# A hybrid SSD and latent-attention decode step: the decay mask added ahead of a biased Exp, the norm weight moved into w_out, and the page table read whole in an earlier stage

## The chip, the cores and the metric

The kernel is one program on one core of a Trainium2 chip. A core has a matrix engine (TensorE, here PE, with its weight loads shown apart as PEld), three engines for the rest (VectorE or DVE, ScalarE or ACT, GpSimd or POOL), and SyncE (SP), which here issues most DMA transfers. Each engine works through its own instructions strictly in the order in which they stand, and waits on semaphores for the others. The metric is device time in microseconds (us) for one execution. Smaller is better. Before the change, the median of three timed runs was 2083.14 us (2076.83 to 2083.86).

## The reference, cut to what matters

Two layers run over a prompt of 1024 tokens and over 8 sequences of 8 new tokens each (64 tokens, the "sample"). Layer 0 is a Mamba-2 SSD mixer with 32 heads in 8 groups, layer 1 is multi-head latent attention (MLA) with a paged cache of 2048 past positions for each sequence. What the change touches of the SSD mixer:

```python
seg = a_cs[..., :, None] - a_cs[..., None, :]
decay = jnp.where(causal, jnp.exp(jnp.where(causal, seg, 0.0)), 0.0)
cb = jnp.einsum('bclgn,bcsgn->bgcls', cc, bc)
y_diag = jnp.einsum('bgrcls,bcsgrp->bclgrp', cb[:, :, None] * decay, xdt)   # xdt = x * dt
...
y = y.reshape(b, t, SSD_D_INNER) * jax.nn.silu(z.astype(F32))
yg = yg * lax.rsqrt(jnp.mean(yg * yg, axis=-1, keepdims=True) + NORM_EPS)
y = yg.reshape(b, t, SSD_D_INNER) * norm_w.astype(F32)
out = jnp.einsum('bte,ed->btd', y.astype(h.dtype), w_out)
```

So for each chunk of 128 tokens and each head, a 128x128 matrix of decays exp(a_cs[t] - a_cs[s]) is masked to s <= t, multiplied with the products of C and B, and multiplied into x * dt. Later the gated result is normalised by groups of 256, multiplied with `norm_w` for each of the 2048 columns, and projected by `w_out`. In layer 1 the sample's queries attend to pages that `page_table` (8 x 16 integers) names; the kernel fetches four pages of a sequence with one indirect transfer, for which each of the 128 partitions needs a row number: partition 32 j + r of item (b, q) needs page_table[b, 4 q + j] * 32 + r.

## The kernel before, in words

All products are made in a fast 32-bit format, with each operand split into a high part (a copy, on ACT) and a low part (the rest, a subtraction on DVE or POOL), and three products in place of one. The helper `split` (L129, L130) does that.

**Layer 0.** The eight SSD groups are handled one behind the other, as a pipeline of two: while `ssd_scan` goes over the nine token tiles of group g (eight of 128 prompt tokens, and the sample's 64), the generator `Group.steps` makes the projections of group g + 1. These are four convolution blocks of three pieces each (24 products into one of two PSUM buffers `pj`, evacuated by ACT at L452 to L455), convolved by DVE at L468, and a SiLU per pair of blocks at L429 (prompt, `acc`) and L430 (sample, `xs`), and then nine gate tiles `z` (L100). `layer_ssd` takes steps of the one as weights of the other allow, and within this a scheduler, which works from its own estimate of durations, lays out each engine's instructions. So the order on the engines isn't that of the code. Ahead of group 0, `ssd_dt` makes for each tile four columns per head in `k.tok`: 0 the cumulated decay exponent `acs`, 1 `dt`, 2 and 3 factors for the state and its output; it also writes `acs` transposed to DRAM as `acs_d`.

A tile of `ssd_scan` goes so. Transposes of x and B into `trp` (L537 to L540); ACT copies x to `xsT` (L542) and splits B; DVE makes `xdt` = x * dt (L555); POOL makes `xdd` = x times column 2 (L558), which is split with ACT's and POOL's help; POOL and ACT split the state S and C; POOL makes `xD` (L567). PE makes `pc` = B C (L569, PSUM tag `cb`, one buffer), and DVE multiplies it with the 0/1 mask into `cbm` (L571). A DMA broadcasts the tile's `acs` row of four heads to all partitions as `M` (L573, two buffers, 256 KB). DVE then does for each head `min(M - acs[s], 0)` (L575, four instructions of 128x128), ACT one Exp over all four heads (L577), DVE one product with `cbm` (L578). PE multiplies `M` with `xdt` into `py` (L582), makes the tile's state `st` (L586) and the part from the old state. DVE and POOL add up and gate `y` (L655 to L661), ACT sums its squares (L662), POOL multiplies it with the norm weight `nw` (L663), and SyncE writes it to `y_d`.

ACT keeps one table of functions at a time. Where Exp follows SiLU or the other way round, a table load stands ahead of it (ACT_TABLE_LOAD, under the line of the function that needs it).

The last group's scan has no projections beside it. Beside it runs `ssd_outproj` over the first eight of 16 row blocks of `w_out`, which `load_wout` loads, copies to `woh` on ACT (L703) and splits into `wol` on DVE and POOL in turn (L704). The second half of the blocks follows behind the scan. `rstd_of` scales with a power step on POOL (L204).

**Layer 1.** `mla_in` normalises the rows of the residual (`norm_steps`: transposes `xtp` with three PSUM buffers, then `hh` on ACT and `hl` on DVE, L235 and L236) and makes gates and latents; there `gather_kpe` fetches the page table as one number per partition (`kpidx`, L1353) and gathers key rows. Then `mla_q` makes the queries, with `Heads` already preparing the first heads, then `Sample.__init__` makes the row numbers: four transfers broadcast every fourth word of the page table to 32 partitions each (L1381), one loads r (`pslot`, L1383), and DVE converts, scales and converts back (L1385 to L1388). Then come the heads of the prompt, and the sample's attention, which uses the row numbers (`ptidx`) in 32 indirect transfers. In these last two stages PE and POOL keep the order of the code.

Of the kernel before, what the change touches and what calls it, by code (L numbers as in the profile page):

```python
# [18 lines left out]
NB = 8  # L19
# [18 lines left out]
SCALE = (NOPE + ROPE) ** -0.5  # L38
NEG = -1e30
GB = 4  # L40
NKT = 4
# [102 lines left out]
def ssd_tiles(k):  # L144
    cp, nc = k.cs, k.nc
    k.masku = cp.tile([128, 128], F32, name="masku")
    k.masks = cp.tile([64, 128], F32, name="masks")
    k.blkm = cp.tile([64, NB], F32, name="blkm")
    k.yssq = cp.tile([128, 9, G], F32, name="yssq")
# [13 lines left out]
def ssd_consts(k):  # L163
    nc, I = k.nc, k.I
    nc.sync.dma_start(k.masku, I["c_masku"])
    nc.sync.dma_start(k.masks, I["c_masks"])
    nc.sync.dma_start(k.blkm, I["c_blkm"])
    for j in range(3):
        nc.sync.dma_start(k.blk3[32 * j : 32 * j + 32], I["c_blkm"][:32, :4])
    nc.gpsimd.memset(k.yssq, 1.0)  # L170
    nc.sync.dma_start(k.dtb, I["ssd_dt_bias"][0].partition_broadcast(128))
    nc.sync.dma_start(k.dsk, I["ssd_d"][0].partition_broadcast(128))
# [162 lines left out]
def ssd_dt(k, pool, psum):  # L335
# [26 lines left out]
    def tokv(j):  # L362
        return k.tok[:, :, j]
# [3 lines left out]

    nc.gpsimd.tensor_copy(tokv(0), v(acs))
    nc.gpsimd.tensor_copy(tokv(1), v(dt))
    nc.vector.tensor_tensor(u, pt[:, :n], acs, op=ALU.subtract)  # L370
# [150 lines left out]
def ssd_scan(k, gr, pools):  # L521
# [4 lines left out]
    hs = slice(4 * g, 4 * g + 4)  # L526
    nw = sp.tile([128, 256], F32, tag="nw", name=f"nw{g}", bufs=1)
    nc.sync.dma_start(nw, I["ssd_norm_w"][0, 256 * g : 256 * g + 256].partition_broadcast(128))
    for i in ORDER[g]:
# [23 lines left out]

        xdt = sp.tile([128, 256], F32, tag="xdt", name="xdt" + tag, bufs=2)
        nc.vector.tensor_tensor(v3(xdt), v3(p[:, 0:256]), hb(1), op=ALU.mult)  # L555
        if not smp:
# [12 lines left out]
        nc.tensor.matmul(pc[:m, :m], B, C, start=True, stop=True)  # L569
        cbm = sp.tile([128, 128], F32, tag="cbm", name="cbm" + tag, bufs=1)  # L570
        nc.vector.tensor_tensor(cbm[:m, :m], pc[:m, :m], (k.masks if smp else k.masku)[:m, :m], op=ALU.mult)  # L571
        M = sp.tile([128, 4, 128], F32, tag="M", name="M" + tag, bufs=2)
        nc.sync.dma_start(M[:m, :, :m], (k.acss_d[hs] if smp else k.acs_d[i, hs]).partition_broadcast(m))  # L573
        for h in range(4):
            nc.vector.tensor_scalar(M[:m, h, :m], M[:m, h, :m], tk[:, 0, 4 * g + h : 4 * g + h + 1], 0.0,  # L575
                                    op0=ALU.subtract, op1=ALU.min)
        nc.scalar.activation(M[:m, :, :m], M[:m, :, :m], AF.Exp)  # L577
        nc.vector.tensor_tensor(M[:m, :, :m], M[:m, :, :m],  # L578
                                cbm[:m, :m].unsqueeze(1).to_broadcast([m, 4, m]), op=ALU.mult)
        py = psum.tile([128, 512], F32, tag="y", name="py" + tag, bufs=PB["y"])  # L580
        for h in range(4):
            nc.tensor.matmul(py[:m, h * 64 : h * 64 + 64], M[:m, h, :m], xdt[:m, h * 64 : h * 64 + 64],  # L582
                             start=True, stop=True)
# [78 lines left out]
        nc.scalar.activation(xD[:m], y[:m], AF.Square, accum_out=k.yssq[:m, i, g : g + 1])  # L662
        nc.gpsimd.tensor_tensor(y[:m], y[:m], nw[:m], op=ALU.mult)  # L663
        nc.sync.dma_start(k.y_d[sl, 256 * g : 256 * g + 256], y[:m])
# [30 lines left out]
def load_wout(k, pool, raws, kks, ws):  # L695
    nc = k.nc
    wo = k.I["ssd_w_out"][0]
    for kk in kks:
# [3 lines left out]
        nc.sync.dma_start(raw, wo[kk * 128 : kk * 128 + 128])  # L702
        nc.scalar.copy(hi, raw)  # L703
        (nc.vector if kk % 2 else nc.gpsimd).tensor_tensor(lo, raw, hi.bitcast(F32), op=ALU.subtract)  # L704
        ws.append((hi, lo))
# [161 lines left out]
def mla_in(k, right, mid):  # L867
    tc, nc, I = k.tc, k.nc, k.I
    k.g_d = k.dram.tile([8, 128, T], F32, name="g_d")
    with ExitStack() as st:  # L870
# [17 lines left out]
        with open_pool(tc, name="kg", bufs=1, side="right") as kg:  # L888
            gk = gather_kpe(k, kg)
            next(gk)  # L890
            for n in range(QG + 8):
                next(gates)
                if n >= QG:
                    next(gk)
# [477 lines left out]


class Sample:
    def __init__(self, k, pool):
        nc, I = k.nc, k.I
        self.k, self.sp = k, None
        pt = pool.tile([128, 32], mybir.dt.int32, name="ptab")
        for j in range(4):
            src = I["page_table"].rearrange("b (q j) -> j (b q)", j=4)[j : j + 1].to_broadcast([32, 32])  # L1380
            nc.sync.dma_start(pt[32 * j : 32 * j + 32], src)  # L1381
        ps = pool.tile([128, 1], F32, name="pslot")
        nc.sync.dma_start(ps, I["c_slot"])  # L1383
        pf = pool.tile([128, 32], F32, name="ptf")
        nc.vector.tensor_copy(pf, pt)  # L1385
# [409 lines left out]
def layer_mla(k):  # L1795
# [3 lines left out]
    with ExitStack() as st:  # L1799
# [27 lines left out]
        hd.open(heads, psum)  # L1827
        sm = Sample(k, qp)
        with tc.manual_schedule(engines={nc.tensor.engine, nc.gpsimd.engine}):
# [65 lines left out]
```

## Time and profile before

| | |
|---|---|
| timed runs | 2076.83, 2083.86, 2083.14 us, median 2083.14 |
| profiled execution | 2079.06 us, of which the span of the kernel's instructions is 2077.3 us |
| instructions on the chip | 33714 |
| PE busy | 1939.1 us, 93% of the span |
| DVE, ACT, POOL busy | 1325.8, 1043.0, 852.6 us |
| granted PE clock, mean | 0.977 of full speed |
| HBM traffic | 152.10 MB read, 53.28 MB written, 99 GB/s |

The profile is of one execution. Times in it count from the first instruction. A row of a group reads: line, engine, operation, output and inputs, shape, count, then busy time, mean duration in ns, and how long the engine stood idle ahead of it and what ended that. A row of the waits reads: engine and instruction, what it waited for, us in total, how often, longest. A row of the windows gives a stretch, with the busy time of PE, weight loads, DVE, ACT and POOL in it. Products on PE overlap, so their busy time is not PE at its peak.

The stages lie so: normalisation and the first group's projections up to 145 us, the scans of groups 0 to 6 up to about 840, the last scan with the first half of the output product up to about 1012, its second half up to about 1125, the input stage of layer 1 up to 1322, queries up to 1420, the prompt's heads up to about 1760, then the sample.

### The profile page before, as it was taken

What the parts mean: (1) busy time and instruction counts of PE and PEld (TensorE: products, weight loads), DVE (VectorE), ACT (ScalarE), POOL (GpSimd) and SP (SyncE); (2) the same over time, 40 slices, a digit from 0 to 9 for tenths busy, and PEclk for the clock granted to TensorE, in tenths of its full rate; (3) what the DMA queues carried; (4) which work ended last, traced back from release to release, by engine and by line L of the source; (5) the groups of instructions that cost most, each with busy time, mean ns of one, the idle gap of its engine ahead of it and who ended that gap; (6) DMA issues with size and microseconds to landing.
All of it is one profiled execution on the core that took longest, in us unless ns stands there. A gap on an engine that the chain in (4) does not pass through costs nothing.

```text
span 2077.3 us, 33714 instructions
## 1 busy us (share of the span) xinstructions
PE 1939.1 (93%) x12001; PEld 1750.3 (84%) x12001; DVE 1325.8 (64%) x2790; ACT 1043.0 (50%) x2288; POOL 852.6 (41%) x1059
## 2 busy tenths in 40 slices
PE   6999999999999999789998999799999999889998
PEld 5898989899999999677777998698888888778887
DVE  4558676767676768865434315366787868776665
ACT  5455555555565656522113314234676767755552
POOL 0337464646664646653000001102333434765541
PEclk9999999999999999889999999899999999999999
DMA  4222323232323241645544332132111212454451
GB/s 145 56 60 62 111 68 109 63 110 66 106 67 109 64 114 44 192 145 168 184 152 128 126 136 86 41 110 79 48 44 43 64 38 77 136 185 134 139 152 39
DMA packets 187631, 207.61 MB, mean 100 GB/s; under 512 B 23260, under 2 KB 153064, under 8 KB 187080
## 3 DMA queue, kind: packets, MB, share of 16 engines
q1 hardware_dynamic: 182408, 185.67, 29.7%
q0 software_dynamic: 4976, 19.66, 3.0%
q8 instruction: 95, 1.56, 0.3%
q14 instruction: 72, 0.59, 0.1%
q10 hardware_dynamic: 80, 0.13, 0.0%
HBM read 152.10 MB, written 53.28 MB: 99 GB/s over the span
## 4 chain that ended last, share of the span: by engine, by line
PE 58%; DVE 15%; DMA 10%; issue 7%; POOL 5%; ACT 4%; SPq 1%; POOLq 0%; DVEq 0%; ACTq 0%
PE pj L88 12%; PE pz L100 9%; PE pq L100 5%; PE pob L100 5%; DMA M<-acs_d 4%; PE poa L100 4%; DVE M L575 3%; DVE acc L468 3%; POOL kvl L1543 2%; PE py L582 2%; PE sc L1212 1%; PE st L1244 1%; PE o L1275 1%; PE st L1246 1%; PE st L1245 1%
## 5 line engine op out<-in xcount | busy, mean ns | idle before, releaser
L88 PE MATMUL pj<-xh,wih 128*128 128x384 f32 (+1 forms) x768 | 254.3, 335 | 9.5 <-ACT xh L235 5.2
L88 PE MATMUL pj<-xl,wih 128*128 128x384 f32 (+1 forms) x768 | 255.5, 333 | 0.0
L88 PE MATMUL pj<-xh,wil 128*128 128x384 f32 (+1 forms) x768 | 254.6, 332 | 0.0
L1258 POOL TENSOR_TENSOR tl<-P,th 128x384 fp32r<-128x384 f32 (+1 forms) x96 | 91.0, 948 | 166.3 <-ACT P L1256 141.3
L468 DVE SCALAR_TENSOR_TENSOR acc<-raw,vec,acc 128x1112 f32<-128x1112 f32 x96 | 147.0, 1535 | 11.9 <-ACT acc L465 11.1
L88 PEld LDWEIGHTS pj<-xh,wih 128*128 128x128 f32 x768 | 145.3, 190 | 10.8 <-ACT xh L235 5.8
L88 PEld LDWEIGHTS pj<-xh,wil 128*128 128x128 f32 x768 | 145.7, 190 | 0.6
L88 PEld LDWEIGHTS pj<-xl,wih 128*128 128x128 f32 x768 | 145.7, 190 | 0.6
L575 DVE TENSOR_SCALAR M<-M,tok 128x128 f32<-128x128 f32 (+1 forms) x288 | 115.3, 458 | 43.8 <-DMA M<-acs_d 35.8
L100 PE MATMUL pz<-wih,xh 128*128 128x256 f32 x504 | 143.0, 287 | 0.0
L100 PE MATMUL pz<-wil,xh 128*128 128x256 f32 (+1 forms) x504 | 142.8, 287 | 0.0
L100 PE MATMUL pz<-wih,xl 128*128 128x256 f32 x448 | 128.2, 286 | 0.0
L1255 ACT ACTIVATE th<-st 128x512 fp32r<-128x512 f32 x192 | 94.3, 491 | 64.3 <-PE st L1251 42.7
L130 DVE TENSOR_TENSOR wil<-wraw,wih 128x512 fp32r<-128x512 f32 x88 | 70.4, 803 | 62.2 <-ACT wih L129 61.5
L1543 POOL TENSOR_TENSOR kvl<-pgr,kvh 128x1024 fp32r<-128x1024 f32 x32 | 78.0, 2439 | 72.4 <-ACT kvh L1542 72.4
L100 PEld LDWEIGHTS pz<-wih,xh 128*128 128x128 f32 x504 | 96.0, 190 | 1.1
L577 ACT ACTIVATE M<-M 128x512 f32<-128x512 f32 (+1 forms) x72 | 43.8, 608 | 103.3 <-DVE M L575 103.0
L1256 ACT ACTIVATE P<-st 128x512 f32<-128x512 f32 x192 | 93.5, 487 | 0.0
L100 PEld LDWEIGHTS pz<-wil,xh 128*128 128x128 f32 (+1 forms) x504 | 92.9, 185 | 0.3
L663 POOL TENSOR_TENSOR y<-y,nw 128x256 f32<-128x256 f32 (+1 forms) x72 | 63.8, 886 | 69.2 <-ACT xD L662 69.0
L1258 DVE TENSOR_TENSOR tl<-P,th 128x512 fp32r<-128x512 f32 x96 | 74.3, 774 | 22.4 <-ACT P L1256 22.1
L582 PEld LDWEIGHTS py<-xdt,M 128*128 128x128 f32 (+1 forms) x576 | 68.9, 189 | 21.9 <-DVE xdt L555 7.5
(819 smaller groups left out, 6438.0 us busy)
## 6 DMA issues: line engine op xcount, KB each, us to landing
wraw<-in_ssd_w_in SPq DMA_DIRECT2D x92, 256.0 KB
M<-acs_d SPq DMA_DIRECT2D x64, 256.0 KB
s<-in_state_ssm SPq DMA_DIRECT2D x32, 256.0 KB
y_d<-y SPq DMA_DIRECT2D x64, 128.0 KB
out_s_ssm<-s SPq DMA_DIRECT2D x32, 256.0 KB
wraw<-in_ssd_w_out SPq DMA_DIRECT2D x16, 512.0 KB
q_d<-qt SPq DMA_DIRECT2D x32, 192.0 KB
qp<-q_d SPq DMA_DIRECT2D x8, 768.0 KB
```

Source lines behind the costliest of these rows:

```text
L88: nc.tensor.matmul(out, a, b, start=(i == 0), stop=(i == n - 1))
L100: nc.tensor.matmul(o, a, b, start=(j == 0), stop=(j == len(ops) - 1))
L130: (eng or nc.vector).tensor_tensor(lo, src, hi.bitcast(F32), op=ALU.subtract)
L468: nc.vector.scalar_tensor_tensor(acc, raw[:, j : j + n], k.convw[j][:, blk : blk + 1], acc, op0=ALU.mult, op1=ALU.add)
L575: nc.vector.tensor_scalar(M[:m, h, :m], M[:m, h, :m], tk[:, 0, 4 * g + h : 4 * g + h + 1], 0.0, op0=ALU.subtract, op1=ALU.min)
L577: nc.scalar.activation(M[:m, :, :m], M[:m, :, :m], AF.Exp)
L582: nc.tensor.matmul(py[:m, h * 64 : h * 64 + 64], M[:m, h, :m], xdt[:m, h * 64 : h * 64 + 64], start=True, stop=True)
L663: nc.gpsimd.tensor_tensor(y[:m], y[:m], nw[:m], op=ALU.mult)
L1255: nc.scalar.activation(th[:, :n], ps[:, :n], AF.Exp, scale=SCALE)
L1256: nc.scalar.activation(P[:, :n], ps[:, :n], AF.Exp, scale=SCALE)
L1258: eng.tensor_tensor(tl[:, :n], P[:, :n], th[:, :n].bitcast(F32), op=ALU.subtract)
L1543: nc.gpsimd.tensor_tensor(rl, raw, rh.bitcast(F32), op=ALU.subtract)
```

## The change

Three edits. (1) The decay: the mask is added to the broadcast row as 0 or -1e30 (`negu`, `negs`, made once by POOL) in one DVE instruction over four heads; Exp then runs per head with a bias per partition, which is column 0 of `k.tok`; that column now holds ln(dt) - acs in place of acs, so that `dt` comes into the Exp and `xdt` goes; the product takes `pc` from PSUM directly, so that `cbm` goes; `py` takes `xsT`. (2) `y` is no longer multiplied with the norm weight on POOL; `load_wout` multiplies the rows of `w_out` with it while it splits them, ACT by a scale, and DVE with one instruction of two operations, for all 16 blocks. (3) The page table is loaded whole into all partitions, and the row numbers are made from it, in the input stage right behind `gather_kpe`'s first part.

```diff
 def ssd_consts(k):
+    for neg, mask in ((k.negu, k.masku), (k.negs, k.masks)):
+        nc.gpsimd.tensor_scalar(neg, mask, -NEG, NEG, op0=ALU.mult, op1=ALU.add)
...
 def ssd_dt(k, pool, psum):
-    nc.gpsimd.tensor_copy(tokv(0), v(acs))
-    nc.gpsimd.tensor_copy(tokv(1), v(dt))
+    lnd = pool.tile([128, n], F32, name="lnd")
+    nc.vector.tensor_scalar(lnd, dt, TINY, None, op0=ALU.max)
+    nc.scalar.activation(lnd, lnd, AF.Ln)
+    nc.vector.tensor_tensor(tokv(0), v(lnd), v(acs), op=ALU.subtract)
...
 def ssd_scan(k, gr, pools):
-    nw = sp.tile([128, 256], F32, tag="nw", name=f"nw{g}", bufs=1)
-    nc.sync.dma_start(nw, I["ssd_norm_w"][0, 256 * g : 256 * g + 256].partition_broadcast(128))
...
-        xdt = sp.tile([128, 256], F32, tag="xdt", name="xdt" + tag, bufs=2)
-        nc.vector.tensor_tensor(v3(xdt), v3(p[:, 0:256]), hb(1), op=ALU.mult)
...
-        cbm = sp.tile([128, 128], F32, tag="cbm", name="cbm" + tag, bufs=1)
-        nc.vector.tensor_tensor(cbm[:m, :m], pc[:m, :m], (k.masks if smp else k.masku)[:m, :m], op=ALU.mult)
         M = sp.tile([128, 4, 128], F32, tag="M", name="M" + tag, bufs=2)
         nc.sync.dma_start(M[:m, :, :m], (k.acss_d[hs] if smp else k.acs_d[i, hs]).partition_broadcast(m))
+        nc.vector.tensor_tensor(M[:m, :, :m], M[:m, :, :m],
+                                (k.negs if smp else k.negu)[:m, :m].unsqueeze(1).to_broadcast([m, 4, m]), op=ALU.add)
         for h in range(4):
-            nc.vector.tensor_scalar(M[:m, h, :m], M[:m, h, :m], tk[:, 0, 4 * g + h : 4 * g + h + 1], 0.0,
-                                    op0=ALU.subtract, op1=ALU.min)
-        nc.scalar.activation(M[:m, :, :m], M[:m, :, :m], AF.Exp)
+            nc.scalar.activation(M[:m, h, :m], M[:m, h, :m], AF.Exp, bias=tk[:, 0, 4 * g + h : 4 * g + h + 1])
         nc.vector.tensor_tensor(M[:m, :, :m], M[:m, :, :m],
-                                cbm[:m, :m].unsqueeze(1).to_broadcast([m, 4, m]), op=ALU.mult)
+                                pc[:m, :m].unsqueeze(1).to_broadcast([m, 4, m]), op=ALU.mult)
...
-            nc.tensor.matmul(py[:m, h * 64 : h * 64 + 64], M[:m, h, :m], xdt[:m, h * 64 : h * 64 + 64],
+            nc.tensor.matmul(py[:m, h * 64 : h * 64 + 64], M[:m, h, :m], xsT[:m, h * 64 : h * 64 + 64],
...
-        nc.gpsimd.tensor_tensor(y[:m], y[:m], nw[:m], op=ALU.mult)
...
 def load_wout(k, pool, raws, kks, ws):
-        nc.scalar.copy(hi, raw)
-        (nc.vector if kk % 2 else nc.gpsimd).tensor_tensor(lo, raw, hi.bitcast(F32), op=ALU.subtract)
+        nw = k.ssdn[:, kk : kk + 1]
+        nc.scalar.activation(hi, raw, AF.Copy, scale=nw)
+        nc.vector.scalar_tensor_tensor(lo, raw, nw, hi.bitcast(F32), op0=ALU.mult, op1=ALU.subtract)
...
             next(gk)
+            page_rows(k, kg)
...
+def page_rows(k, pool):
+    nc, I = k.nc, k.I
+    pt = pool.tile([128, NB * NPG], mybir.dt.int32, name="ptab")
+    nc.sync.dma_start(pt, I["page_table"].rearrange("b p -> (b p)").partition_broadcast(128))
+    ps = pool.tile([128, 1], F32, name="pslot")
+    nc.sync.dma_start(ps, I["c_slot"])
+    pf = pool.tile([128, 32], F32, name="ptf")
+    for j in range(4):
+        r = slice(32 * j, 32 * j + 32)
+        nc.vector.tensor_copy(pf[r], pt[r].rearrange("p (x j) -> p j x", j=4)[:, j])
+    nc.vector.tensor_scalar(pf, pf, 32.0, ps, op0=ALU.mult, op1=ALU.add)
+    k.ptidx = k.cm.tile([128, 32], mybir.dt.int32, name="ptidx")
+    nc.vector.tensor_copy(k.ptidx, pf)
...
 class Sample:
-    def __init__(self, k, pool):
-        nc, I = k.nc, k.I
+    def __init__(self, k):
         self.k, self.sp = k, None
-        pt = pool.tile([128, 32], mybir.dt.int32, name="ptab")
-        for j in range(4):
-            src = I["page_table"].rearrange("b (q j) -> j (b q)", j=4)[j : j + 1].to_broadcast([32, 32])
-            nc.sync.dma_start(pt[32 * j : 32 * j + 32], src)
-        ps = pool.tile([128, 1], F32, name="pslot")
-        nc.sync.dma_start(ps, I["c_slot"])
-        pf = pool.tile([128, 32], F32, name="ptf")
-        nc.vector.tensor_copy(pf, pt)
-        nc.vector.tensor_scalar(pf, pf, 32.0, ps, op0=ALU.mult, op1=ALU.add)
-        self.idx = pool.tile([128, 32], mybir.dt.int32, name="ptidx")
-        nc.vector.tensor_copy(self.idx, pf)
+        self.idx = k.ptidx
```

More of the change, by code (lines that the diff above doesn't have):

```diff
@@ L39 @@
 NEG = -1e30
+TINY = 1e-37
 GB = 4
@@ L147, in ssd_tiles @@
     k.masks = cp.tile([64, 128], F32, name="masks")
+    k.negu = cp.tile([128, 128], F32, name="negu")
+    k.negs = cp.tile([64, 128], F32, name="negs")
     k.blkm = cp.tile([64, NB], F32, name="blkm")
@@ L1827, in layer_mla @@
         hd.open(heads, psum)
-        sm = Sample(k, qp)
+        sm = Sample(k)
         with tc.manual_schedule(engines={nc.tensor.engine, nc.gpsimd.engine}):
```

## The prediction

> **What bounds the kernel now.** I read the page first (busy shares), then busy time and clock by stretch, then what TensorE (PE) waits for in the stretches that the change touches.
>
> ```profile
> span 2077.3 us, 33714 instructions
> PE 1939.1 (93%) x12001; PEld 1750.3 (84%) x12001; DVE 1325.8 (64%) x2790; ACT 1043.0 (50%) x2288; POOL 852.6 (41%) x1059
> ```
>
> ```profile
> 145.00:840.00 695.00, 667.86 (x4856) 643.14 (x4855) 511.14 (x1014) 393.87 (x895) 420.21 (x620) 1.00 0.30 85
> 840.00:1012.00 172.00, 150.34 (x751) 121.71 (x749) 112.16 (x181) 55.68 (x121) 84.19 (x87) 0.90 0.53 173
> 1332.00:1347.00 15.00, 0.00 (x0) 0.00 (x0) 2.06 (x8) 0.58 (x1) 0.00 (x0) 0.59 0.28 74
> 1347.00:1352.00 5.00, 4.80 (x17) 4.68 (x18) 3.38 (x17) 2.98 (x8) 0.54 (x1) 0.53 0.30 111
> ```
>
> The columns are: length, busy time of PE, weight loads, DVE, ACT and POOL, granted clock, DMA share, GB/s. PE bounds the whole; nothing that the change removes is PE work. So it can earn only where PE stands still or runs at a low clock: 27 us in the group scans (145 to 840), 22 us in the last scan with the first half of the output product (840 to 1012, clock 0.90), and one hole of 15 us at 1332 in which no engine does much.
>
> **The page table.** What the hole is made of, from the waits of 1320 to 1352 and SyncE's timeline:
>
> ```profile
> DVE ptf L1385 <- DMA ptab<-in_page_table: 16.9, 1, 16.9
> PE vp L88 <- DVE pq L112: 15.4, 1, 15.4
> ```
>
> ```profile
> 1321.51 10.49 SPq L1381 DMA_DIRECT2D ptab<-in_page_table  x4
> ...
> 1335.08 6.29 SPq L1383 DMA_DIRECT2D pslot<-in_c_slot  x1
> ```
>
> Four transfers that pick every fourth word keep SyncE's queue for 10.5 us. DVE reaches the conversion of the table early and waits 16.9 us for it; behind it in DVE's queue stand the split `cql` and the fold of `pq`, and PE waits 15.4 us for that fold. After the hole PE runs at clock 0.53 until 1352. The change takes the four transfers, `pslot` and the conversion out of this place. What is then late next: PE's own stream ran up to 1332, ACT and DVE have the fold's few instructions (2.06 and 0.58 us busy in the hole) to do, and what stands behind the table on SyncE, weights among it, starts 10 us earlier. So I count all of the 15.4 us, and for the clock 0.47 of 5 us, 2.3 us. **Minus 17.7 us**, bounds minus 20 (the queue behind is also freer) and minus 11 (a backlog of DVE and ACT that the hole had absorbed shows up instead).
>
> What is added: in the changed kernel's built order one broadcast load of the whole table (128 rows of 512 B) and `pslot` stand on SyncE right behind the `kpidx` load, and on DVE four copies, the scaling and the last conversion stand behind the eighth `hl` split of the second row block, ahead of the third block's first.
>
> ```profile
> L1353 SPq DMA_DIRECT2D kpidx<-in_page_table x1: 422/422/422, 1149.7 to 1149.7; - x1
> 1153.37 1.17 POOL L1355 DMA_INDIRECT kprows<-in_cache_kpe,kpidx  x1 [8.57 <-DMA kpidx<-in_page_table]
> 1152.68 0.55 DVE L236 SCALAR_TENSOR_TENSOR hl<-xtp,vec,hh 128x320 fp32r<-128x320 f32 x1 [1.86 <-ACT hh L235]
> ```
>
> `kpidx` is issued at 1149.7 and its reader starts at 1153.4, 3.7 us later. The two new loads issue 0.4 and 0.8 us after it, so DVE gets them near 1154.5 and goes on about 2 us later than 1152.68. Queued behind it: eight `hl` splits; for them waits PE, which has three transpose buffers to run ahead with. PE would wait some 0.7 us; bounds 0 and 2.5. **Plus 0.7 us.**
>
> **The group scans, 145 to 840.**
>
> ```profile
> PE st L88 <- ACT xddh L129: 11.1, 14, 1.4
> PE py L582 <- DVE xdt L555: 6.0, 7, 1.6
> PE py L582 <- DVE M L578: 3.3, 14, 0.6
> PE py L88 <- POOL Sl L130: 3.3, 6, 0.9
> PE st L88 <- POOL xddl L130: 2.3, 7, 0.4
> ```
>
> ```profile
> L575 DVE TENSOR_SCALAR M<-M,tok 128x128 f32<-128x128 f32 x256 | 103.8, 464 | 35.9 <-DMA M<-acs_d 35.8
> L578 DVE TENSOR_TENSOR M<-M,cbm 128x512 f32<-128x512 f32 x64 | 51.9, 812 | 14.4 <-ACT M L577 13.7
> L571 DVE TENSOR_TENSOR cbm<-cb,masku 128x128 f32<-128x128 f32 x64 | 17.8, 279 | 0.0
> L555 DVE TENSOR_TENSOR xdt<-trp,tok 128x256 f32<-128x256 f32 x64 | 26.3, 411 | 0.0
> L577 ACT ACTIVATE M<-M 128x512 f32<-128x512 f32 x64 | 40.4, 632 | 88.2 <-DVE M L575 87.9
> L663 POOL TENSOR_TENSOR y<-y,nw 128x256 f32<-128x256 f32 (+1 forms) x72 | 63.8, 886 | 69.2 <-ACT xD L662 69.0
> ```
>
> DVE per full tile now: 4 x 0.464 + 0.279 + 0.411 + 0.812 = 3.36 us. After: the mask addition and the product with `pc`, both 128x512, 0.81 each by the row of the old product: 1.62. DVE loses 1.74 us per tile, POOL 0.89 us and its wait for the square (69 us in all), and eight `nw` loads go. All of it lies beside PE; it is worth only what it takes off the PE waits above, 26 us. Of these, `xdt` goes (6.0), but `py` then waits for the product: I count 4. For `xddh`, the row that matters is ACT's order: at 474.27 it stands behind the Exp, which waits for four `M` steps; in the built order it stands ahead of the four Exps and of the Silu. I count 7 of 11.1; of the two POOL waits, 2 of 5.6. Minus 13.
>
> ACT pays. Prices from these rows:
>
> ```profile
> L1256 ACT ACTIVATE P<-st 128x512 f32<-128x512 f32 x96 | 56.8, 592 | 0.0
> L1486 ACT ACTIVATE P<-sc,nm 128x512 f32<-128x512 f32 x32 | 22.0, 688 | 63.1 <-DVE nm L1483 58.9 <-DVE mn L1480 4.2
> L577 ACT ACT_TABLE_LOAD x21 | 26.9, 1283 | 3.0 <-DMA M<-acs_d 2.6
> 471.90 0.37 ACT L542 COPY xsT<-trp 128x256 f32<-128x256 f32 x1
> 472.16 0.27 ACT L129 CAST BTh<-trp 128x128 fp32r<-128x128 f32 x1
> ...
> 474.80 0.39 ACT L129 CAST xddh<-xdd 128x256 fp32r<-128x256 f32 x1
> 475.21 1.28 ACT L429 ACT_TABLE_LOAD   x1
> 476.50 1.92 ACT L429 ACTIVATE acc<-acc 128x2048 f32<-128x2048 f32 x1
> 478.68 0.31 ACT L430 ACTIVATE xs<-acc 128x128 f32<-128x128 f32 x1
> 478.89 0.41 ACT L662 ACTIVATE xD<-y 128x256 f32<-128x256 f32 x1
> 744.12 3.67 PE pj L88 x21
> 477.97 1.10 PE py L582 x8
> 479.07 0.41 PE py L88 x3
> ```
>
> A 128x128 activation from SBUF takes 0.31, a bias per partition adds 0.688 - 0.592 = 0.10, and neighbours overlap by 0.10 (478.68 to 478.89): four Exps take 3 x 0.31 + 0.41 = 1.34 us against 0.632. That is 0.7 a tile, some 6.3 a group with the sample tile. The built order also has 12 more table loads than before, two in each of six groups, because the four Exps of one tile now stand between the two Silus of a pair: 2 x 1.28 = 2.6. Together 8.9 us a group on an engine that is busy 394 of 695 us. Does it reach PE? In that place the copies that free the two `pj` buffers now stand at most 8.9 us apart (xsT 0.37, BTh 0.27, xddh 0.39, three loads 3.85, Silu 1.92, Exps 1.34, xs 0.31, square 0.41). PE needs, between them, two pieces of 24 products (8.4 us at 3.67 for 21) and one tile's `py` (1.5): 9.9. It fits by 1 us, without the Exps' wait for `M`. I take 1 us a group, 6 in all; bounds 0 and 8.9 a group. **Net minus 7 us**, bounds minus 26 and plus 36.
>
> One rule of the Trainium skill bears on the DVE sum. "SBUF — State Buffer", section "Who interferes with whom", says that a DVE instruction with two SBUF inputs and a GpSimd instruction that reads SBUF lock each other out, and that one with a single SBUF input outside the two-port modes does not. By it the addition keeps the 0.81, which the old product with two SBUF inputs has, and the new product, with `pc` in PSUM, is an estimate of 0.68 (the rows of `cbm` and `xdt`, one input in PSUM each, give 0.279 at 128 and 0.411 at 256, so 0.132 for 128 more): 1.49 a tile instead of 1.62, and the sum 8 us of DVE less, beside PE either way.
>
> **The last scan and the output product, 840 to 1012.**
>
> ```profile
> PE poa L100 <- ACT woh L703: 2.9, 1, 2.9
> PE cb L569 <- DVE cbm L571: 2.7, 3, 1.8
> L704 DVE TENSOR_TENSOR wol<-wraw,woh 128x1024 fp32r<-128x1024 f32 x8 | 15.3, 1910 | 2.2 <-ACT woh L703 2.0
> ```
>
> DVE saves 9 x 1.74 = 16 us here and takes over eight `wol` from POOL, 8 x 1.9 = 15. Even. The loads of `w_out` no longer wait for POOL, whose `wol` stands behind its power step: I count the 2.9 us of `woh` as gone, and 2 us of the rest, where the state and the scan's products come sooner. The 2.7 of `cbm` I leave: `pc` (one buffer) is now held until the product is done, so `cb` of the next tile waits for that instead. **Minus 5 us**, bounds minus 18 (nearly all of the 22, some clock) and plus 10 (DVE's queue blocked by `wol` that waits for its load).
>
> Nothing else moves by more than noise: `lnd` is two steps more once, ahead of the first group, and spares two POOL copies; the two mask tiles are made by POOL before POOL has scan work; and behind 1352 PE and POOL keep their order. Were that cover gone, each would cost under 1 us, once.
>
> **Sum.** -17.7 + 0.7 - 7 - 5 = -29 us. The profiled execution took 2079.1 (span 2077.3 and 1.8 around it); it lies 4.1 under the median of 2083.1, and the four times average 2080.7. 2080.7 - 29 = **2052 us**.
>
> **Rivals.**
> 1. *Only the hole goes.* The order on PE was laid out anew and its waits return at other places, as `py` on the product. For it: the waits are small and many. -17 gives 2063. Chance 0.22.
> 2. *All waits of the scans go*, -26 and -18 beside -17, with ACT in its gaps: 2020 to 2026. ACT's 301 idle us of 695 speak for it, the 1 us of slack against. 0.12.
> 3. *ACT becomes the bound of the groups (slower).* Place: the copies out of `pj` behind three table loads and four Exps. It decides when the 8.9 us there grow past 9.9, so as soon as the Exps wait over 1 us for `M`; the change as a whole turns slower when a group loses over 2.4 us (17 in 7). At its full price, 8.9 in 7 groups, +62 - 17: 2126. Against it: ACT now idles 88 us for `M`, which comes sooner after. 0.07.
> 4. *The wait moves with the table.* If `ptab` or `pslot` is as slow at 1150 as at 1322 to 1345, DVE stands 10 to 17 us with eight `hl` behind it, and PE stops after three buffers. Against it: 128 runs of 512 B, not 4096 single words. Then -17 shrinks to about -3, with the scans' -12: 2066. 0.09.
> 5. *A table switch empties ACT first.* If each of the three loads took as long again, the 8.9 us would become 12.7, 2.8 over, in six groups +17: 2069. In the trace the load starts at 475.21 right behind work that ends at 475.19, and the Silu follows at 476.50: no such gap. 0.03. The Trainium skill, "ScalarE: Activation LUTs", section "What ACT_TABLE_LOAD costs", puts a switch at 1283 ns and a drain of about 1380 ns; the load agrees with this trace, and the drain does not show in it.
>
> The forecast has the remaining 0.47. The range reaches from half of rival 2 to rival 5: 2030 to 2073, and leaves out rival 3 and the tails. A difference of 0.5%, 10.4 us, is about what can be told from no change. Faster than 2072.7: nearly all of the forecast and rival 2, most of rivals 1 and 4: 0.84. Within: 0.09. Slower, rival 3: 0.07.
>
> **What would show it.** Right: no stretch without PE near 1315, granted clock 1.0 through it; at 1150 a DVE wait for `ptab` or `pslot` near 2 us; in the scans no wait of PE for `xdt`, less for `xddh`, and 27 and 6 table loads on the lines of Exp and of the second Silu; ACT busy some 60 us more. Wrong: PE waits for ACT's copies of `pj` in each group (rival 3), a DVE wait over 5 us at 1150 (rival 4), or the waits of 145 to 840 still summing to 26 us (rival 1).

## The result, and the profile after

The changed kernel takes 2049.3 us (median of four runs, 2047.6 to 2053.4) against 2081.8 (2076.8 to 2083.9): 0.985 of the time, 95% interval 0.9825 to 0.9875. The forecast was 2052. Its profiled execution took 2050.8, so 28.3 less than that of before. The page of the kernel after:

```profile
span 2049.0 us, 33431 instructions
PE 1929.3 (94%) x12001; PEld 1749.0 (85%) x12001; DVE 1227.9 (60%) x2443; ACT 1102.9 (54%) x2517; POOL 806.5 (39%) x979
```

DVE lost 98 us of work, POOL 46, ACT gained 60. The stretches that answer to those of before, with their ends moved as the stream moved (length, busy time of PE, weight loads, DVE, ACT and POOL, clock, DMA share, GB/s):

```profile
145.00:840.00 695.00, 668.52 (x4863) 653.18 (x4863) 430.63 (x704) 449.20 (x1101) 399.17 (x559) 0.99 0.30 84
840.00:1003.00 163.00, 143.99 (x744) 116.50 (x742) 97.16 (x150) 59.71 (x141) 60.37 (x69) 0.94 0.56 181
1313.00:1344.00 31.00, 30.97 (x193) 30.00 (x191) 21.91 (x64) 14.18 (x30) 7.00 (x8) 1.00 0.39 128
```

The last row lies where the hole was, in the stream's own time: PE works through it at clock 1.0. The first shows the surprise: in the group scans PE is busy for 668.5 of 695 us, much as before (667.9), although DVE is busy 80 us less there. The waits of PE in this stretch (what waited for what, total us, times, longest):

```profile
PE pj L89 <- ACT raw L459: 14.3, 6, 2.9
PE st L89 <- ACT xddh L130: 6.4, 6, 1.8
PE st L89 <- POOL xddl L131: 2.4, 4, 1.2
```

The waits for `xdt` (6.0) and nearly all for `M` (3.3, now 0.2) are gone and `xddh` fell from 11.1 to 6.4, but a wait that was not there stands on top: for ACT's copy out of `pj`, once in each of six groups. All waits of PE in this stretch together are 26.1 us, against 26.4 before. Between 840 and 1003 `woh` (2.9) and `cbm` (2.7) have gone, but for 0.3, and others lead:

```profile
PE st L89 <- POOL xddl L131: 5.0, 3, 2.6
PE poa L101 <- ACT yha L130: 4.2, 6, 2.6
```

And the prices of the new instructions, from the groups of 145 to 840, and of `wol` from those of 840 to 1003:

```profile
L561 POOL TENSOR_TENSOR xdd<-xsT,tok 128x256 f32<-128x256 f32 x54 | 53.3, 988 | 52.8 <-ACT xsT L547 50.1 <-PE st L89 2.7
L575 DVE TENSOR_TENSOR M<-M,negu 128x512 f32<-128x512 f32 x56 | 50.0, 893 | 25.7 <-DMA M<-acs_d 25.7
L579 DVE TENSOR_TENSOR M<-M,cb 128x512 f32<-128x512 f32 x55 | 37.1, 675 | 4.0 <-ACT M L578 4.0
L578 ACT ACT_TABLE_LOAD x26 | 33.4, 1283 | 0.4
L437 ACT ACT_TABLE_LOAD x6 | 7.7, 1283 | 0.1
```

```profile
L705 DVE SCALAR_TENSOR_TENSOR wol<-wraw,vec,woh 128x1024 fp32r<-128x1024 f32 x16 | 21.5, 1347 | 7.0 <-ACT woh L704 7.0
```

**Marks in the trace.** To place a gain, I use four: *G*, the last of the transposes `ctp` of the last group (near the end of the group scans), *A*, the last product `poa` (end of the output product's first half), *K*, the first `pk` (input stage of layer 1) and *L*, the first `lo` (end of the sample). Ahead of *G* PE makes the same number of products in every kernel (5355 to 5359 in the records), and so ahead of *A* (6354 or 6355). All in us, from one profiled execution of every kernel that ran (the others are described below), with its median, and the ratio to the runs of the kernel before that were timed beside it (medians 2078.9 to 2082.1).

| kernel | median | ratio (interval) | G | A - G | K - A | L - K |
|---|---|---|---|---|---|---|
| before | 2081.8 | | 810.0 | 201.2 | 228.7 | 815.9 |
| after | 2049.3 | 0.985 (0.9825-0.9875) | 808.9 | 193.3 | 229.1 | 796.5 |
| page table alone | 2065.7 | 0.9929 (0.9906-0.9953) | 813.8 | 201.7 | 230.0 | 797.8 |
| decay and norm weight, no table | 2068.0 | 0.9929 (0.9900-0.9957) | 804.1 | 196.0 | 229.5 | 815.5 |
| norm weight alone | 2050.2 | 0.9862 (0.9842-0.9882) | 790.2 | 191.6 | 227.0 | 813.8 |
| decay alone | 2078.3 | 0.9995 (0.9978-1.0013) | 818.5 | 193.3 | 229.5 | 814.8 |
| after, one SiLU | 2033.4 | 0.9765 (0.9741-0.9789) | 796.1 | 193.1 | 227.6 | 800.2 |
| after, one Exp | 2071.7 | 0.9961 (0.9942-0.9979) | 820.7 | 193.1 | 230.3 | 795.3 |
| after, `xdd` on DVE | 2038.0 | 0.9793 (0.9776-0.9809) | 796.7 | 191.2 | 227.6 | 801.9 |
| after, one SiLU and `xdd` on DVE | 2023.9 | 0.9721 (0.9702-0.9740) | 785.2 | 193.3 | 228.1 | 800.9 |
| norm weight and table | 2038.6 | 0.9806 (0.9778-0.9833) | 789.8 | 199.5 | 228.9 | 796.9 |
| the same, `xdt` removed by ln dt | 2048.9 | 0.9860 (0.9836-0.9883) | 805.6 | 196.6 | 228.1 | 794.3 |
| the same, one SiLU, `xdd` on DVE | 2051.8 | 0.9859 (0.9838-0.9880) | 801.1 | 194.0 | 238.2 | 797.0 |
| norm weight alone, `xD` made twice | 2060.4 | 0.9912 (0.9883-0.9941) | 797.6 | 200.4 | 227.6 | 811.7 |

Three pairs in it differ in the page table only and have the same order of PE's instructions in layer 0, so each shows one order twice: before and table alone, after and "no table", norm weight alone and with table. Their scatter is 0.4 to 4.8 us in G and up to 7.9 in A - G. What that last scatter is shows in the same 1029 products of the norm-weight pair, first alone, then with the table (on the first row PE stands 20.2 us, on the second 20.8):

```profile
787.00:982.00 195.00, 174.79 (x1029) 147.01 (x1027) 127.40 (x234) 75.38 (x163) 79.86 (x94) 0.96 0.51 161
```

```profile
787.00:990.00 203.00, 182.16 (x1029) 152.45 (x1028) 126.89 (x234) 74.97 (x163) 80.22 (x94) 0.92 0.49 155
```

The granted clock was 0.92 instead of 0.96, and the products took 7.4 us more. So below, differences of 5 us in a stretch decide nothing, and pairs are taken by their mean.

It helps to part a stretch into the time in which PE stands idle and the time that its products take. From the windows view, in us, with the granted clock:

| kernel | 145 to G: idle | products | clock | G to A: idle | products | clock |
|---|---|---|---|---|---|---|
| before | 27.1 | 637.9 | 1.00 | 21.7 | 179.5 | 0.92 |
| page table alone | 27.4 | 641.4 | 0.99 | 21.2 | 180.5 | 0.90 |
| after | 26.4 | 637.5 | 0.98 | 19.1 | 174.2 | 0.95 |
| decay and norm weight, no table | 29.0 | 630.1 | 1.00 | 22.5 | 173.5 | 0.96 |
| norm weight alone | 14.6 | 630.6 | 1.00 | 20.2 | 171.4 | 0.96 |
| norm weight and table | 14.4 | 630.4 | 1.00 | 20.8 | 178.7 | 0.92 |
| decay alone | 34.2 | 639.3 | 0.99 | 18.0 | 175.3 | 0.95 |

On the means of the pairs the whole change leaves PE's idle time as it was in both stretches (27.3 and 27.7 us up to G, 21.4 and 20.8 behind it). What it gains there lies in the time that the products take, and with one and the same order that time moved by 7.4 us with the clock.

### The profile page after: what moved, and what is told of

Read it like the earlier page. It is cut to its first block, busy times and chain, and to the rows that moved or that the text cites. A ratio compares the mean times of both kernels' runs of the same rounds, so it can differ in the third digit from the quotient of the medians.

```text
span 2049.0 us, 33431 instructions
## 1 busy us (share of the span) xinstructions
PE 1929.3 (94%) x12001; PEld 1749.0 (85%) x12001; DVE 1227.9 (60%) x2443; ACT 1102.9 (54%) x2517; POOL 806.5 (39%) x979
## 4 chain that ended last, share of the span: by engine, by line
PE 63%; DMA 10%; ACT 8%; DVE 7%; POOL 6%; issue 5%; SPq 1%; POOLq 0%; ACTq 0%; DVEq 0%
PE pj L89 17%; PE pz L101 7%; PE pq L101 5%; PE pob L101 5%; PE poa L101 4%; PE py L583 2%; PE p L101 2%; DMA M<-acs_d 2%; PE sc L1214 1%; PE st L1246 1%; POOL kvl L1549 1%; PE pk L101 1%; PE o L1277 1%; PE st L1248 1%; PE st L1247 1%
## 5 line engine op out<-in xcount | busy, mean ns | idle before, releaser
L475 DVE SCALAR_TENSOR_TENSOR acc<-raw,vec,acc 128x1112 f32<-128x1112 f32 x96 | 143.5, 1498 | 23.4 <-ACT acc L472 22.5
L578 ACT ACTIVATE M<-M,tok 128x128 f32<-128x128 f32 (+1 forms) x288 | 91.1, 386 | 66.0 <-DVE M L575 65.5
L1260 DVE TENSOR_TENSOR tl<-P,th 128x512 fp32r<-128x512 f32 x96 | 73.9, 769 | 22.1 <-ACT P L1258 21.9
L561 POOL TENSOR_TENSOR xdd<-xsT,tok 128x256 f32<-128x256 f32 x64 | 60.9, 952 | 65.0 <-ACT xsT L547 60.1
L101 PEld LDWEIGHTS pz<-wih,xl 128*128 128x128 f32 x448 | 86.1, 192 | 0.2
L575 DVE TENSOR_TENSOR M<-M,negu 128x512 f32<-128x512 f32 x64 | 56.7, 886 | 33.6 <-DMA M<-acs_d 33.5
```

The source lines that it names most:

```text
L101: nc.tensor.matmul(o, a, b, start=(j == 0), stop=(j == len(ops) - 1))
L475: nc.vector.scalar_tensor_tensor(acc, raw[:, j : j + n], k.convw[j][:, blk : blk + 1], acc, op0=ALU.mult, op1=ALU.add)
L561: nc.gpsimd.tensor_tensor(v3(xdd), v3(xsT), hb(2), op=ALU.mult)
L575: nc.vector.tensor_tensor(M[:m, :, :m], M[:m, :, :m], (k.negs if smp else k.negu)[:m, :m].unsqueeze(1).to_broadcast([m, 4, m]), op=ALU.add)
L578: nc.scalar.activation(M[:m, h, :m], M[:m, h, :m], AF.Exp, bias=tk[:, 0, 4 * g + h : 4 * g + h + 1])
L1260: eng.tensor_tensor(tl[:, :n], P[:, :n], th[:, :n].bitcast(F32), op=ALU.subtract)
```

## Experiments

My theory after the two traces: the table is worth its hole; between 840 and 1012 it is `w_out`; in the groups, the decay edit's savings are eaten by its table loads on ACT. The rivals: POOL or the new order is what keeps PE, and the loads only stand by.

**1. The page table alone** (before, with that part of the diff).

> The kernel before with the page-table edit alone. Theory (the two traces put 19.3 us between the end of the input stage and the first rows of the sample's work, clock included, and 0.4 us against it): about 19 us less than before, 0.991 of it, with no PE wait and clock 1.0 near 1325, and the group scans ending at 805 as before. Rival (part of the gain only appeared because the stages ahead had moved, or ACT's and DVE's backlog shows up): 11 us less or under.

Measured: 2065.7, 16.4 less than the 2082.1 of before beside it: short of the 19 of the theory, and well over the 11 of the rival. L - K is 797.8 against 815.9, and the longest wait of PE where the hole was is

```profile
PE pq L100 <- ACT qt L1013: 1.8, 1, 1.8
```

The edit pays without the others. Over all kernels, L - K is 811.7 to 815.9 in the five without it (mean 814.3) and 794.3 to 801.9 in the nine with it (mean 797.9): 16.5 us.

**2. Decay and norm weight, no table** (after, with the old `Sample.__init__`).

> The changed kernel with the old page-table code, so the decay and norm-weight edits alone. Theory: 9 to 10 us less than before (0.9955), all of it between 840 and 1012, the hole of 15 us at its old place, the scans of groups 0 to 6 ending at 805 to 806. Rival (the edits help each other): over 13 us less, or no gain.

Measured: 2068.0, 14.2 less: more than the 9 to 10 of the theory, and over the line of 13 that I had drawn for the rival. But with an interval of 9 to 21 us this doesn't decide it, and the 16.4 of experiment 1 and these 14.2 add up to 30.6, where the whole change gave 32.5: nothing here says that the edits help each other. A - G is 196.0, and G 804.1 where the same order had 808.9. The hole is back. The new wait for `raw` repeats to the tenth:

```profile
PE pj L89 <- ACT raw L459: 14.2, 6, 2.9
```

**3. One SiLU for prompt and sample columns.**

```diff
-        nc.scalar.activation(acc[:, :, :SEQ], acc[:, :, :SEQ], AF.Silu)
-        nc.scalar.activation(xs..., bass_window(acc, ...), AF.Silu)
+        nc.scalar.activation(acc, acc, AF.Silu)
+        nc.scalar.copy(xs..., bass_window(acc, ...))
```

> The changed kernel with one SiLU per pair of blocks over prompt and sample columns together (xs is then a copy, which needs no table), so that no Exp can come between the two: 12 table loads fewer, as many as before the change; the four Exps per tile stay. Theory (the copies out of pj were late because three table loads stood ahead of them): PE's wait for raw falls from 14.3 us to under 4, the six stretches of half clock in the scans go for the most part, the last group's first projections end 10 to 15 us earlier than 805.6, and the whole takes 2034 to 2040. Rival A (the four Exps themselves, or their waits for M, keep ACT): the wait for raw stays over 9 us and the time within 5 us of 2049. Rival B (PE waits elsewhere instead, on POOL's xddl above all, with the half clock behind it): the wait for raw goes but the time falls by less than 6.

Measured: 2033.4, G at 796.1. Table loads are back at the number of before, and PE's waits between 145 and 840 became

```profile
PE st L89 <- POOL xddl L131: 10.7, 14, 2.6
PE pj L89 <- ACT raw L458: 7.2, 5, 1.6
PE st L89 <- ACT xddh L130: 4.3, 4, 1.6
```

The theory's time came, its mechanism half: `raw` fell to 7.2, not under 4, and POOL's `xddl` rose to 10.7. So the loads cost time, and POOL was the next thing late (rival B's place, not its size). The profiled execution was the slowest of the four (2040.0), so the marks show less than the median gained.

**4. One Exp over four heads, bias and mask on DVE.**

The indices are shortened in this cut:

```diff
-        nc.vector.tensor_tensor(M, M, negu, op=ALU.add)
         for h in range(4):
-            nc.scalar.activation(M[h], M[h], AF.Exp, bias=tk[:, 0, h])
+            nc.vector.scalar_tensor_tensor(M[h], M[h], tk[:, 0, h], negu, op0=ALU.add, op1=ALU.add)
+        nc.scalar.activation(M, M, AF.Exp)
```

> The changed kernel with one Exp over four heads, as before the change; the bias and the mask are added by DVE, four instructions of 128x128 with two operations each in place of one of 128x512. It needs 10 table loads fewer. Theory (loads): about like one SiLU alone, 2034 to 2042, as ACT loses 0.7 us a tile more but DVE gains 1 us a tile. Rival A (the four Exps): this one gains 10 or more and the one-SiLU kernel under 5. Rival B (PE's waits come back on DVE or POOL): within 6 us of 2049.

Measured: 2071.7 (ten runs, 2062.4 to 2080.8), against theory and both rivals' size, 22 slower than after. The wait for `raw` went (0.8 us), but:

```profile
PE st L89 <- ACT xddh L130: 8.7, 9, 3.8
PE st L89 <- POOL xddl L131: 7.3, 6, 1.2
...
PE py L583 <- DVE M L579: 4.8, 6, 0.9
```

```profile
L576 DVE SCALAR_TENSOR_TENSOR M<-M,tok,negu 128x128 f32<-128x128 f32 x216 | 96.4, 499 | 37.3 <-DMA M<-acs_d 37.3
```

DVE's step is 4 x 0.499 = 2.0 us instead of 0.893, and PE now waits 4.8 us for `M`: an engine busy 62% can still be late. The 8.7 us of `xddh` are not due to ACT's order: in eight of these nine waits ACT's cast itself stood waiting for POOL's `xdd`. How the 22 us come about is shown only in part.

**5. The norm weight alone** (before, with that part of the diff).

> The kernel before with the norm-weight edit alone (POOL's product with nw goes, w_out is scaled while it is split, all of wol on DVE). Theory: most of the 8 us that the changed kernel gains between 840 and 1012 come from here, as wol no longer stands in POOL's queue and the wait for woh (2.9 us) goes; in the groups nothing beyond the scatter between executions (about 5 us); 2073 to 2078. Rival (the gain comes from the decay): under 3 us between 840 and 1012.

Measured: 2050.2, 31 us less, as much as the whole change, with the hole still in it. Of it 10 lie in A - G (6 on the mean with experiment 9), as expected, and some 20 in the groups, where I expected none. PE's two longest waits from 145 to 840, and POOL's longest of the kernel before in the same stretch (second fence):

```profile
PE s0p L629 <- DMA s<-in_state_ssm: 6.1, 7, 1.1
PE st L88 <- ACT xddh L129: 5.0, 7, 1.2
```

```profile
POOL y L663 <- ACT xD L662: 64.2, 38, 2.5
```

The waits for `xddh`, `xdt`, `M`, `Sl` and `xddl` all fall (26.0 to some 8), and the one for the load of `s` comes on top. By the table of idle times, some 13 of the 22 us of G (on the means of the pairs) are PE standing less, and 9 are the time of its products. In the kernel before, POOL stood 64 us at the norm product for ACT's square, in some places with the next tile's `xdd` behind it, and that would be the obvious reason. The trace of before does not bear it out for the largest wait. One of six places alike, on POOL and on ACT:

```profile
471.20 1.26 POOL L663 TENSOR_TENSOR y<-y,nw 128x256 f32<-128x256 f32 x1 [2.33 <-ACT xD L662]
...
473.54 0.61 POOL L558 TENSOR_TENSOR xdd<-xsT,tok 128x256 f32<-128x256 f32 x1
```

```profile
474.27 0.63 ACT L577 ACTIVATE M<-M 128x512 f32<-128x512 f32 x1 [1.83 <-DVE M L575]
474.80 0.39 ACT L129 CAST xddh<-xdd 128x256 fp32r<-128x256 f32 x1
```

POOL's `xdd` is late, but done at 474.15, and the cast still stands behind the Exp, which waits for DVE. So it is in 12 of the 14 waits for `xddh`; one ends behind ACT's square, and one (1.05 us) on POOL's `xdd`. Two more things came with the edit: another order on every engine, and shorter instructions on DVE, which is what `M` waits for (the steps L575 took 428 ns on the mean and not 464, the convolutions 1437 and not 1535). The gain is measured; its path to PE is not shown.

**6. The decay alone.**

> The kernel before with the decay edit alone. Theory: the waits for ACT's raw stand here at about 14 us in six places, as in the changed kernel, those for xdt are gone; the groups end within 5 us of 805; between 840 and 1012 a gain under 3 us; 2076 to 2083. Rival (the decay is what gains in the output product): over 5 us between 840 and 1012.

Measured: 2078.3, not to be told from before. G is 818.5, 6.6 later than the mean of before's pair, and not within 5 us of 805; A - G is 193.3, 8 less, which is the rival's side: between 840 and 1012 either edit alone brings 6 to 8, and both together no more. The wait for `raw` is there without the norm weight:

```profile
PE pj L89 <- ACT raw L459: 12.7, 6, 2.9
```

**7. `xdd` on DVE** (after, `xdd` multiplied from the transposes in PSUM).

```diff
-            nc.gpsimd.tensor_tensor(v3(xdd), v3(xsT), hb(2), op=ALU.mult)
+            nc.vector.tensor_tensor(v3(xdd), v3(p[:, 0:256]), hb(2), op=ALU.mult)
```

> The changed kernel with xdd made by DVE from the transposes in PSUM instead of by POOL from SBUF. POOL loses about 0.95 us a tile (0.62 before the change: it runs beside DVE's addition of the mask, which has two inputs in SBUF), DVE gains 0.41. Theory (POOL's lengthened xdd makes xddh and xddl late): the waits for xddh and xddl fall from 8.8 to under 4 us, the wait for raw stays near 14 as the table loads stay; the group scans end 4 to 8 us earlier, 2041 to 2046. Rival (POOL's lengthening is hidden): within 3 us of 2049, the waits for xddh and xddl as before.

Measured: 2038.0, G at 796.7, 10 earlier than the pair of after, so more than the theory said, and the wait for `raw` did not stay. The order now has 64 table loads in place of 62, and yet:

```profile
PE py L583 <- DVE M L579: 10.2, 7, 1.7
PE st L89 <- POOL xddl L131: 3.5, 8, 0.6
...
PE pj L89 <- ACT raw L459: 1.2, 5, 0.3
```

`xddh` (1.7) and `raw` both go, so it takes more than loads to make `raw` late. What it takes is in ACT's timeline of the kernel after, in one group (start, duration, and in brackets what it waited for), with PE's, POOL's and DVE's in fences of their own:

```profile
364.72 0.47 ACT L459 COPY raw<-pj 128x384 f32<-128x384 f32 x1
...
368.70 0.41 ACT L130 CAST xddh<-xdd 128x256 fp32r<-128x256 f32 x1 [3.08 <-POOL xdd L561]
369.13 1.28 ACT L436 ACT_TABLE_LOAD   x1
370.42 1.91 ACT L436 ACTIVATE acc<-acc 128x2048 f32<-128x2048 f32 x1
372.36 1.28 ACT L578 ACT_TABLE_LOAD   x1
373.65 1.28 ACT L578 ACTIVATE M<-M,tok 128x128 f32<-128x128 f32 x4
374.94 1.28 ACT L437 ACT_TABLE_LOAD   x1
...
376.86 0.46 ACT L459 COPY raw<-pj 128x384 f32<-128x384 f32 x1
```

```profile
377.36 0.45 PE L89 MATMUL pj<-xh,wih 128*128 128x384 f32 x1 [2.58 <-ACT raw L459]
```

```profile
365.21 1.81 POOL L131 TENSOR_TENSOR Sl<-S,Sh 128x256 fp32r<-128x256 f32 x1
366.98 1.69 POOL L561 TENSOR_TENSOR xdd<-xsT,tok 128x256 f32<-128x256 f32 x1
368.63 0.61 POOL L570 TENSOR_TENSOR xD<-xsT,dsk 128x256 f32<-128x256 f32 x1
```

```profile
363.20 3.23 DVE L475 SCALAR_TENSOR_TENSOR acc<-raw,vec,acc 128x1112 f32<-128x1112 f32 x2
366.35 0.41 DVE L657 TENSOR_TENSOR y<-py,tok 128x256 f32<-128x256 f32 x1
366.68 1.51 DVE L475 SCALAR_TENSOR_TENSOR acc<-raw,vec,acc 128x1112 f32<-128x1112 f32 x1
368.12 0.41 DVE L658 TENSOR_TENSOR y<-y,py 128x256 f32<-128x256 f32 x1
368.45 0.68 DVE L579 TENSOR_TENSOR M<-M,cb 128x512 f32<-128x512 f32 x1
```

The two copies stand 12.1 us apart: 3.1 us of waiting for POOL's `xdd`, then the row of three loads, Silu and Exps. POOL was late because its `Sl` and `xdd`, beside DVE's convolution (and not beside the addition of the mask, as I had expected), took 1.81 and 1.69; `xD`, an operation of the same shape, took 0.61 when DVE had gone on to instructions that read PSUM (`py`, `cb`). In this group both the wait and the loads stand ahead of the copy. Taking either away (experiments 3 and 7) gives about 10 us of G. Experiment 8 gives the sum of the two, so they are not two conditions of one and the same loss.

**8. One SiLU and `xdd` on DVE.**

> One SiLU per pair and xdd on DVE together. Theory: the 10.7 us of waits for xddl and 4.3 for xddh of the one-SiLU kernel fall to under 6, and the time from 2033 to 2022 to 2028. Rival (DVE's 0.41 us a tile more makes M or the convolutions late, or PE's waits move to s0p and raw): within 4 us of 2033.

Measured: 2023.9, the fastest, 25 us under after; G at 785.2, 21 earlier than after's pair. `xddl` and `xddh` together wait 3.4 us, `raw` 2.0, and what leads is a load:

```profile
PE s0p L631 <- DMA s<-in_state_ssm: 3.6, 5, 2.4
```

**9. Norm weight and table, decay as before.**

> The kernel before with the norm-weight and the page-table edits, the decay left as it was. The norm-weight edit alone gave 2050.2, and the page table takes 18 to 19 us from the end of the input stage to the sample. Theory (the decay edit, as written, costs time beside the norm weight): 2029 to 2034, some 17 less than the changed kernel; the groups end near 787. Rival (what the norm weight gained alone was one lucky order, and a new one falls back): 2040 or more.

Measured: 2038.6, 10.6 under after (9 by the ratios), so the decay edit as written, with the order that comes with it, does cost time beside the other two. It lies between the 2029 to 2034 of the theory and the rival's 2040: in the profiled execution G repeats (789.8), the table gives its 17, and the 7.4 us lost to the clock, shown above, lie in A - G. That the other runs lost as much is not shown.

**10. The same, with `xdt` removed by ln dt** (indices shortened).

```diff
-        nc.vector.tensor_scalar(M[h], M[h], acs[h], 0.0, op0=ALU.subtract, op1=ALU.min)
+        nc.vector.tensor_scalar(M[h], M[h], lnd_minus_acs[h], lnd[h], op0=ALU.add, op1=ALU.min)
```

> The kernel of the norm-weight and page-table edits, and of the decay edit only the part that removes xdt: DVE does min(M + (ln dt - acs), ln dt) for each head with the two columns, in the same four instructions, then one Exp, the product with cbm as before, and py takes xsT. No mask addition with two inputs in SBUF, no Exp per head. Theory (of the decay edit the removed xdt is worth a few us, and the four Exps with their table loads and the mask addition are what cost): 2024 to 2031, 50 table loads as before. Rival (the xdt was hidden, or Ln brings a new order): 2031 to 2040.

Measured: 2048.9, 10 slower than without it, beyond the rival. DVE has 18 us less to do in all, no engine more than 14 us more, and the number of loads is the same; but the order came out anew, and PE waits in it from 145 to 840 for

```profile
PE st L89 <- POOL xddl L131: 10.3, 11, 2.4
PE st L89 <- DVE BTl L131: 5.9, 5, 1.5
```

G is 15.8 later than in experiment 9. The edit and the order that came with it can't be told apart here, but less work on DVE came out slower.

**11. Norm weight alone, `xD` made twice.** POOL's line of `xD` stands there twice.

> The norm-weight edit alone, with xD made twice by POOL (the second time the same values), 0.65 to 0.7 us of POOL work a tile that waits for no other engine, in place of the 0.89 that the edit took away. Theory (what the norm weight cost was its place in POOL's queue, a wait of 64 us in all for ACT's square with the next tile's work behind it): 2050 to 2057. Rival (it was POOL's work): 2064 or more.

Measured: 2060.4, between the two: 10 of the 31 us are lost again, 7.6 of the 22 in G, with 54 of the 67 us of POOL work back (839.4 busy against 785.5). Some 40% of the gain would then be POOL's work, if the new order of this kernel cost nothing, and the rest the wait in its queue or the order that came with it; these I did not separate.

**12. Experiment 10 with one SiLU and `xdd` on DVE.**

> The kernel with xdt removed by ln dt, with one SiLU per pair and with xdd made by DVE from PSUM besides. Theory (the same two remedies that took 25 us off the changed kernel): 2016 to 2025. Rival (they only undid what the decay edit had brought): within 4 us of the kernel without them, or slower, as DVE has 0.41 us a tile more.

Measured: 2051.8, on the rival's side. The remedies do not carry over: G is 4.5 earlier than in 10, with PE now waiting for `M`, and K - A is 10 longer, where the page table came at a bad moment. DVE waited 6.3 us there for `ptab`. PE's wait in the groups:

```profile
PE py L581 <- DVE M L577: 14.3, 13, 2.2
```

## Why the prediction came out right, and where it was wrong

The number held: -28.3 us between the profiled executions against -29. For the page table, more than half of it, the mechanism held too. For the rest it was luck: the waits that I had counted as going went, others came in their place, and the time was gained elsewhere. Two of the three signs that I had named for being wrong are there: PE waits for ACT's copies of `pj` in each group, and the waits of 145 to 840 still sum to 26 us. Term by term:

- **The page table, -17.7**: -16.5, between the bounds and by the mechanism given. The hole and the slow 5 us behind it are gone, and no wait of PE over 1.8 us came in their place.
- **Its new place, +0.7**: K - A is 228.7 on the mean of the eight kernels with it (without experiment 12) and 228.5 without it: nothing that can be measured. DVE waited 2.9 us for the broadcast load in the changed kernel. Rival 4 was right that this wait depends on its moment: it was 6.3 us in experiment 12.
- **The last scan and output product, -5**: -6.8 on the means of the pairs, but not as counted. `woh` went, and the `cbm` wait, which I had left standing, and other waits came: PE stands idle for 21.7 and 21.2 us before, 19.1 and 22.5 after. The gain lies in the time of the products, at clock 0.95 and 0.96 in place of 0.92 and 0.90; why the clock was higher is not shown. `wol` takes 1.35 us and not the 1.9 of its row before. Nor is it the norm weight's alone: the decay alone brings as much.
- **The groups, -7**: -5.4 on the means of the pairs, whose members differ by 3.8 and 4.8, so the size is hardly more than noise, and the mechanism failed: PE's idle time up to G did not fall by 7 us, it is 27.3 on the mean before and 27.7 after. Both parts of the sum were wrong. The step that failed first is the pricing of the norm weight: "of the two POOL waits, 2 of 5.6". The norm weight alone moves G by -21.9, and the decay, for which I counted 11 of gain and 6 of cost, alone by +6.6 and beside the norm weight by +16.5. I had the row of POOL's product with "its wait for the square (69 us in all)" and called it work beside PE. How it reaches PE stays open: the reading of `xddh` by ACT's order was right for 12 of its 14 waits, as experiment 5 shows.
- **"It fits by 1 us"**: it did not. I summed 8.9 us of ACT's work between two copies out of `pj` and found 12.1, because `xddh` in that row waits 3.1 us for POOL. That is rival 3's mechanism, in its place and in six groups, at 2.4 us a group and not 8.9: I had made its condition a wait of the Exps for `M`, and another wait, the cast's 3.1 us for `xdd`, met it. The 1 us a group, 6 in all, became 14.3 in all.
- **Rival 1**, only the hole goes and PE's waits return at other places, describes PE's idle time in both stretches and the groups of the profiled pair (G 810.0 and 808.9), but not the time, which came out 14 us under its 2063. **Rival 2** did not come. **Rival 5**: each load takes 1283 ns, and what follows starts right behind it (370.42 after 369.13 + 1.28), as in the trace of before. The drain that the Trainium skill ("ScalarE: Activation LUTs", section "What ACT_TABLE_LOAD costs") adds does not show here either.
- **The DVE prices**: the product with `pc` took 0.675 us, so the 0.68 worked out beside the rule of the Trainium skill ("SBUF — State Buffer", section "Who interferes with whom") was nearer than the 0.81 of my sum. The addition took 0.893 and not 0.81. The other side of that rule, that POOL pays too, I left out: `xdd` went from 0.615 us on the mean to 0.988.

What stays open: each edit of the scan made the scheduler lay out a new order, and experiment 10 came out 15.8 us later in G with 18 us less of work on DVE and 14 more on POOL. The effects of the decay and the norm weight above are those of edit and order together. That G repeats to 5 us within the pairs says that an order's time is its own; it does not say what another order of the same work would take. And why the products took less time in the changed kernel is not shown beyond the granted clock.

## What to carry to other kernels

Sum a queue's work between two deadlines with its waits in it: 8.9 us of work were 12.1 here, and 1 us of slack was none. When a sum agrees with the clock, try its parts alone: here an error of 20 us on the norm weight and one as large on the decay beside it had cancelled. Part each gain into the time in which the engine that bounds stands idle and the time that its work takes: waits that go can come back under other names. And before a long wait in a queue is called the reason, follow it to the instruction that the bounding engine waits for, and look at what that one stood behind.

## What the runs showed of the hardware

- POOL's elementwise instructions of 128x256 took 0.61 to 1.81 us within one group (experiment 7). The long ones ran beside DVE's convolution, which reads two tiles in SBUF, and the short one beside DVE instructions that read PSUM.
- One order of instructions, run twice, differed by 7.4 us in 1029 products at granted clocks of 0.96 and 0.92, while PE stood idle for nearly the same time (20.2 and 20.8 us). What lowered the clock is not shown.
- Four DVE instructions of 128x128 with two SBUF tiles and a column took 4 x 0.499 us (experiment 4), one of 128x512 with two SBUF tiles 0.893 (the changed kernel).
